# A hybrid trunk step: the copies of the first expert matrix in pieces of 1 MB that begin behind the memory's keys and values, and these keys and values in panels of 512 columns

## The chip, the cores and the metric

The kernel runs on one core of a Trainium2 chip. A core has five engines that run in parallel, each with its own order of instructions: TensorE (PE in the profile; its loads of the standing operand are PEld), VectorE (DVE), ScalarE (ACT), GpSimd (POOL) and SyncE (SP), and 16 DMA engines that they feed through queues. The metric is the device time of one execution in microseconds, less is better. Engines wait for each other by semaphores; a DMA that is issued from an engine's queue (SPq, ACTq, POOLq) stands in that engine's order like any other instruction, so what stands behind it waits as long as the issue does.

## The reference

One layer of a trunk, in float32, for a prompt of 256 tokens and 8 samples of 8 tokens (64 tokens), which share all weights. D is 2048.

```
mk, mv = mem_kv(mem_prompt, norm_mem_kv, w_mem_k, w_mem_v)    # 256 memory tokens: rmsnorm, then @ wk and @ wv
m = mixer(rmsnorm(x), ...)                                    # h = xn @ w_in; SSD scan, short convolution; @ w_out
x = x + m
x = x + mem_attend(rmsnorm(x), mem_k, mem_v, w_mem_q, w_mem_o)  # 4 heads of 512
x = x + peer(rmsnorm(x), w_peer_q, sub_keys, peer_u, peer_v)    # 8 heads, best 16 of 128 x 128 experts
```

The prompt attends to the keys and values that `mem_kv` has just made (they are outputs too); each sample attends to its own cached ones (`cache_mem_k`, `cache_mem_v`, 256 tokens each). In `peer` every token takes 128 of 16384 experts: `act = gelu(x . u[e])`, and the result is the sum of `g * act * v[e]`. `peer_u` and `peer_v` are 16384 x 2048 matrices, 134 MB each.

## The kernel before

**Arithmetic.** A matrix product in float32 is made of three matmuls of a rounded type (fp32r): each operand is split into a high part H and the rest L, and H*H, L*H and H*L are summed in PSUM. The split of a weight tile of 128x512 is one ScalarE instruction (`split`, L233: H is the rounded copy) and one VectorE subtraction (L234: L). So a unit of weights goes from DRAM into a room, through ScalarE, through VectorE, and then into 12 matmuls or so.

**The stages** follow each other along one stream: memory keys and values (two GEMMs of 256 tokens by 2048x2048), the input projection `w_in` with the SSD scan and the short convolution among it, the output projection `w_out`, the memory queries and attention over memory, `w_mem_o`, the queries of the experts (`w_peer_q`), the stage that multiplies all tokens with all of `peer_u`, and the stage that does the same with `peer_v`. TensorE, VectorE and ScalarE follow the order in which the program writes their instructions.

**The stream** (class `Stream`). A unit of work goes through four steps: its load is issued; three units later (WA) it is prepared, which is its split; it stands in a queue of up to six units (GD; four for units of attention, KVB - 1); and it is popped, which writes its matmuls. With every pop the stream also takes one step of a generator `steady` (L521), and a number of steps, by a rate, of each side job (norms, scans, softmax). So the units of the GEMMs set the place of all other work. There are four rooms of 512 KB for weight loads (WB; all weight loads are issued by SyncE) and seven buffers each for H and L (HLB).

**The keys and values** (L523 to L533). Each of the two matrices is done in 8 panels of 256 columns. A panel is 8 units; a unit takes two of the 16 row blocks k of the weight, and a load of 512 KB serves two units (rows of 1 KB, L293 to L300; the first two rooms are filled ahead, L402). The memory tokens are the standing operand here (`tok=True`): for each of 2 blocks of tokens and 2 blocks k there are three matmuls of 128x256 (L312 to L314). At the end of a panel two evictions by ScalarE (L530) scale the rows into a tile of 256 KB, and GpSimd issues the DMA that stores it (L532). During the first units a side job `mem_in` at rate 1.5 (L437) transposes and splits the memory tokens. In all there are 128 units.

**The copies.** `ordered_rows` (L509 to L519) copies `peer_u` into a DRAM buffer `u_d`, with its elements in another order: 512 copies of 256 KB each, DRAM to DRAM, issued from ScalarE's queue (L518), in pieces of 2 KB (512 columns). `u_d[i]` holds the 128 experts of row i, so that 32 partitions hold a quarter of the columns, and the stage that reads it can make its transpose by VectorE's 32x32 blocks. The copies begin after 48 pops, and then go at 0.92 of a copy for each pop. What is left at the end of attention is issued at once (`drain(strm.steady)`). The stage that reads them takes `u_d[i]` (1 MB, contiguous, 8 KB per partition) by one DMA of SyncE for each of 128 rows (L1760).

**Attention.** For each of 4 heads there are 8 key tiles of the samples and one of the prompt, and as many value tiles. A key tile comes by four DMAs of SyncE in pieces of 512 B (L1199), a value tile by one DMA of GpSimd (L1202), into four buffers (KVT); tiles are fetched three ahead. VectorE turns key tiles (L1223), ScalarE makes the high part (KH, L1232), VectorE or GpSimd the rest (KL, L1233). Units of `w_mem_q` and `w_mem_o` stand between the units of attention.

**Semaphores of the DMAs.** The DMAs that SyncE and ScalarE issue share eight semaphores (DMAHW0 to DMAHW7 in the orders below), taken in turn in the order in which the program writes the DMAs. A DMA that takes a semaphore again carries a wait for the landing of the one before it there, eight back, unless its engine has seen that landing already.

Of the kernel before, what the change touches and what calls it, by code (L numbers as in the profile page):

```python
# [11 lines left out]
F32 = mybir.dt.float32  # L12
# [3 lines left out]
AF = mybir.ActivationFunctionType  # L16
# [3 lines left out]
P = 128  # L20
D = 2048
KC = D // P
TP = 256
# [109 lines left out]
def wait(n):  # L133
    for _ in range(n):
        yield 1
# [11 lines left out]
def step(ctx, tc, ins, outs, dbg=None, stop=None):  # L147
# [23 lines left out]
    def ps(name="ps"):  # L171
        return psp.tile([P, 512], F32, tag="ps", name=name)
# [38 lines left out]
    def wfree(w):  # L211
        for r in rooms:
            if r[1] is w:
                r[1:] = None, next(turn)
# [16 lines left out]
    def split(h, l, src):  # L231

        S.activation(h, src, AF.Copy)  # L233
        V.tensor_tensor(l, src, h.bitcast(F32), ALU.subtract)  # L234
# [34 lines left out]
    def gain(j, k):  # L269
        return GAIN[:, 16 * j + k:16 * j + k + 1]  # L270

    def gemm(w2d, col0, ncol, ah, al, n, evac, ktot=KC, row0=0, tok=False, w0=None):


        nm = n // P if tok else (ncol + P - 1) // P
        pts = []
        box = {}

        def unit(kq):
            def load():  # L280
                if kq in (0, 2) and w0 is not None:
                    box["room", kq + 1] = w0[kq // 2]
                    box["w"] = w0[kq // 2].rearrange("p (k n) -> p k n", n=ncol)
                elif kq % 2 == 0:
                    w = box["room", kq + 1] = wtile(box["room", kq - 1] if kq % 4 else None)
                    wv = w[:, 0:4 * ncol].rearrange("p (k n) -> p k n", n=ncol)
                    r0 = row0 + kq * 2 * P
                    nc.sync.dma_start(wv, w2d[r0:r0 + 4 * P, col0:col0 + ncol].rearrange("(k p) n -> p k n", p=P))
                    box["w"] = wv
                box["w", kq] = box["w"]  # L290

            def prep():
                h, l = high(), low()  # L293
                hv = h[:, 0:2 * ncol].rearrange("p (k n) -> p k n", n=ncol)
                lv = l[:, 0:2 * ncol].rearrange("p (k n) -> p k n", n=ncol)
                q = kq % 2
                split(hv, lv, box.pop(("w", kq))[:, 2 * q:2 * q + 2])
                if q == 1:
                    wfree(box.pop(("room", kq)))
                box[kq] = (hv, lv)  # L300

            def comp():
                if kq == 0:
                    pts.extend(ps(f"pg{m}") for m in range(nm))
                hv, lv = box.pop(kq)
                for m in range(nm):
                    for j in range(2):
                        k = kq * 2 + j
                        st, sp = k == 0, k == ktot - 1
                        if tok:  # L310
                            out, a0, a1 = pts[m][:, 0:ncol], ah[:, k, m * P:(m + 1) * P], al[:, k, m * P:(m + 1) * P]
                            PE.matmul(out, a0, hv[:, j], start=st, stop=False)  # L312
                            PE.matmul(out, a0, lv[:, j], start=False, stop=False)
                            PE.matmul(out, a1, hv[:, j], start=False, stop=sp)  # L314
                        else:
                            c0, c1 = m * P, min(ncol, m * P + P)
                            out = pts[m][0:c1 - c0, 0:n]
                            PE.matmul(out, hv[:, j, c0:c1], ah[:, k, 0:n], start=st, stop=False)  # L318
                            PE.matmul(out, hv[:, j, c0:c1], al[:, k, 0:n], start=False, stop=False)  # L319
                            PE.matmul(out, lv[:, j, c0:c1], ah[:, k, 0:n], start=False, stop=sp)  # L320
# [77 lines left out]
    for i in range(2):  # L398
        for b in range(2):
            cols = slice(1024 * i, 1024 * i + 1024)  # L400
            nc.sync.dma_start(mem[b][:, cols], mem_prompt[0, b * P:(b + 1) * P, cols])
        nc.sync.dma_start(w0[i], w_mem_k[0, 512 * i:512 * i + 512, 0:256].rearrange("(k p) n -> p k n", p=P))  # L402
    squares = [pM.tile([P, 4], F32, name=f"sq{b}") for b in range(2)]

    def half_square(b, i):
# [28 lines left out]
        half_square(b, 0)  # L434
    next(mi)
    next(mi)
    strm.side(mi, 1.5)  # L437

    def x_norm():
        gb = gain_rows(norm_mix[0])  # L440
# [65 lines left out]
            yield 1  # L506
        S.activation(alog, alog, AF.Exp)

    def ordered_rows(first, last, share):  # L509

        n, done_ = 0, 0.0
        for i in range(first, last):
            for b in range(4):
                while done_ < 1:
                    done_ += share
                    yield 1
                done_ -= 1
                nc.scalar.dma_start(u_d[i, 32 * b:32 * b + 32].rearrange("p (a d) -> p a d", a=4),  # L518
                                    peer_u[0, i * P:(i + 1) * P, 512 * b:512 * b + 512].rearrange("(a p) d -> p a d", p=32))  # L519

    strm.steady = chain(wait(48), ordered_rows(0, P, 0.92))  # L521
    side = strm.side(chain(x_norm(), vectors(), histories()), 0.3)
    for w, dst in ((w_mem_k, p_mem_k), (w_mem_v, p_mem_v)):  # L523
        d2 = dst[0, 0].rearrange("m h d -> m (h d)")
        for c in range(8):
            def evac(m, pt, c=c, d2=d2, box={}):
                if m == 0:
                    box["o"] = pM.tile([P, 2, 256], F32, tag="kvo", bufs=2, name="kvo")
                o = box["o"]
                S.activation(o[:, m], pt[:, 0:256], AF.Copy, scale=mem_scale[m])  # L530
                if m == 1:
                    nc.gpsimd.dma_start(d2[:, c * 256:(c + 1) * 256].rearrange("(m p) n -> p m n", p=P), o)  # L532
            gemm(w[0], c * 256, 256, MH, ML, TP, evac, tok=True, w0=w0 if w is w_mem_k and c == 0 else None)  # L533
    strm.then(lambda: drain(side))
    strm.then(strm.sides.clear)
    strm.then(pMs.close)
# [1522 lines left out]
```

## Time and profile before

| | |
|---|---|
| median of 3 runs | 3337.76 us (3334.13 to 3353.14) |
| the profiled execution | 3339.66 us, its span 3338.0 us |
| mean granted TensorE clock | 0.982 |
| busy: TensorE, VectorE, ScalarE, GpSimd | 96%, 72%, 49%, 41% of the span |
| keys and values | some 11 to 242 us |
| input and output projection | some 242 to 1250 us |
| memory queries and attention | some 1250 to 1530 us |
| stage that reads `u_d` | some 1760 to 2608 us |
| copies into `u_d` | issued from 115.0 to 1243.4 us |

The profile's page gives the busy time of each engine, and then the span in 40 equal slices (83 us each) with a digit for the busy tenths of each. A row of windows gives the busy time of each engine in one stretch, the granted clock, the busy share of the 16 DMA engines, and GB/s. A row of the timeline is one instruction: its start, its duration, the engine, the line, what it writes and reads, and in brackets how long its engine was idle before and what ended that. A row of the waits sums, for two kinds of instructions, how long one waited for the other: total, times, longest. Matmuls are pipelined, so that the spacing of their starts and not their duration is what each costs.

### The profile page before, as it was taken

The numbers are of one execution on the slowest core, as the hardware profiler recorded it, in microseconds if no ns is written. First come the engines' busy times: TensorE is split into PE (matmuls) and PEld (weight loads), VectorE is DVE, ScalarE is ACT, GpSimd is POOL, SyncE is SP. The second block draws the span as 40 slices with busy tenths as digits, with TensorE's granted clock in tenths as the row PEclk, the third lists the DMA queues.
The fourth block names the chain that finished last, engine by engine and source line by source line (L and its number), as shares of the span: only waits on it lengthen the run. The fifth ranks groups of instructions, "written<-read, shape, count | busy, mean of one in ns | idle before, by whom it ended". The sixth has DMA issues, their size and how long they took to land. (4 is left out here: it accounts for less than half of the span.)

```text
span 3338.0 us, 59412 instructions
## 1 busy us (share of the span) xinstructions
PE 3196.1 (96%) x21357; PEld 3006.4 (90%) x21357; DVE 2387.4 (72%) x4558; ACT 1641.4 (49%) x3235; POOL 1363.9 (41%) x1431
## 2 busy tenths in 40 slices
PE   6998999999999999989999989899999999999998
PEld 6998899999999999878999989899999887878886
DVE  4535676665566447776687899988886688878886
ACT  4544453333355345555444444366665454545554
POOL 0001121111100001231127988888888555656652
PEclk8998999999999999989999999999999999999999
DMA  8897788988799889676686577787899899999996
GB/s 200 263 328 249 227 277 275 288 273 270 250 321 291 278 290 228 188 227 209 169 217 219 188 287 282 262 310 280 316 328 317 284 333 330 337 320 333 339 312 203
DMA packets 497652, 909.43 MB, mean 272 GB/s; under 512 B 46767, under 2 KB 325447, under 8 KB 471844
## 3 DMA queue, kind: packets, MB, share of 16 engines
q1 hardware_dynamic: 369068, 562.95, 51.2%
q0 software_dynamic: 54560, 208.44, 18.7%
q10 hardware_dynamic: 73728, 134.25, 13.2%
q8 instruction: 167, 2.74, 0.3%
q14 instruction: 129, 1.06, 0.1%
HBM read 849.40 MB, written 190.05 MB: 311 GB/s over the span
## 5 line engine op out<-in xcount | busy, mean ns | idle before, releaser
L234 DVE TENSOR_TENSOR L<-W,H 128x512 fp32r<-128x512 f32 x1320 | 909.9, 717 | 392.5 <-ACT H L233 376.8
L233 ACT ACTIVATE H<-W 128x512 fp32r<-128x512 f32 x1320 | 802.9, 625 | 756.0 <-PE acc L1962 264.7
L1790 POOL TENSOR_TENSOR L<-tt,H 128x512 fp32r<-128x512 f32 x490 | 630.3, 1315 | 94.2 <-ACT H L1787 83.8
L318 PE MATMUL pg<-AH,H 128*128 128x320 f32 (+1 forms) x1872 | 592.5, 316 | 19.7 <-ACT H L233 19.7
L1808 PE MATMUL pu<-XP,L 128*128 128x256 f32 x2048 | 586.7, 286 | 25.0 <-POOL L L1790 22.6
L1806 PE MATMUL pu<-XP,H 128*128 128x256 f32 x2048 | 588.8, 288 | 4.0 <-ACT H L1787 4.0
L320 PE MATMUL pg<-AH,L 128*128 128x320 f32 (+1 forms) x1872 | 584.0, 312 | 1.6 <-DVE L L234 1.5
L1807 PE MATMUL pu<-XP,H 128*128 128x256 f32 x2048 | 582.5, 284 | 0.0
L319 PE MATMUL pg<-AL,H 128*128 128x320 f32 (+1 forms) x1872 | 582.2, 311 | 0.0
L1808 PEld LDWEIGHTS pu<-XP,L 128*128 128x128 f32 x2048 | 395.5, 193 | 31.0 <-POOL L L1790 27.6
L1778 DVE STREAM_TRANSPOSE tt<-W 128x512 f32<-128x512 f32 x512 | 338.3, 691 | 105.2 <-POOL L L1790 99.6
L1787 ACT ACTIVATE H<-tt 128x512 fp32r<-128x512 f32 x512 | 309.9, 626 | 203.0 <-DVE tt L1778 186.5
L1961 PE MATMUL acc<-L,wt 128*128 128x512 f32 x1024 | 401.0, 392 | 6.9 <-DVE L L234 6.9
L1960 PE MATMUL acc<-H,wt 128*128 128x512 f32 x1024 | 400.4, 391 | 3.0 <-ACT H L233 3.0
L1806 PEld LDWEIGHTS pu<-XP,H 128*128 128x128 f32 x2048 | 396.4, 194 | 5.0 <-ACT H L1787 4.8
L1962 PE MATMUL acc<-H,wt 128*128 128x512 f32 x1024 | 400.3, 391 | 0.0
L1807 PEld LDWEIGHTS pu<-XP,H 128*128 128x128 f32 x2048 | 396.1, 193 | 0.0
L318 PEld LDWEIGHTS pg<-AH,H 128*128 128x128 f32 (+1 forms) x1872 | 354.3, 189 | 26.7 <-ACT H L233 22.3
L320 PEld LDWEIGHTS pg<-AH,L 128*128 128x128 f32 (+1 forms) x1872 | 353.6, 189 | 5.9 <-DVE L L234 5.1
L319 PEld LDWEIGHTS pg<-AL,H 128*128 128x128 f32 (+1 forms) x1872 | 354.4, 189 | 2.2
L1909 POOL TENSOR_TENSOR at<-at,G 128x108 f32<-128x108 f32 x192 | 173.2, 915 | 256.4 <-DMA at<-act_d 198.8
L1961 PEld LDWEIGHTS acc<-L,wt 128*128 128x128 f32 x1024 | 193.4, 189 | 49.8 <-DVE L L234 9.3
(487 smaller groups left out, 5706.2 us busy)
## 6 DMA issues: line engine op xcount, KB each, us to landing
u_d<-in_peer_u_dram ACTq DMA_DIRECT2D x512, 256.0 KB, 6.2
W<-u_d SPq DMA_DIRECT2D x128, 1024.0 KB, 5.3
W<-in_peer_v_dram SPq DMA_DIRECT2D x256, 512.0 KB, 7.1
W<-in_w_in_dram SPq DMA_DIRECT2D x176, 512.0 KB, 7.2
W<-in_w_out_dram SPq DMA_DIRECT2D x64, 512.0 KB, 7.1
W<-in_w_mem_k_dram SPq DMA_DIRECT2D x32, 512.0 KB, 5.0
W<-in_w_mem_v_dram SPq DMA_DIRECT2D x32, 512.0 KB, 8.4
W<-in_w_mem_q_dram SPq DMA_DIRECT2D x32, 512.0 KB, 7.0
```

The source lines that it names most:

```text
L233: S.activation(h, src, AF.Copy)
L234: V.tensor_tensor(l, src, h.bitcast(F32), ALU.subtract)
L318: PE.matmul(out, hv[:, j, c0:c1], ah[:, k, 0:n], start=st, stop=False)
L319: PE.matmul(out, hv[:, j, c0:c1], al[:, k, 0:n], start=False, stop=False)
L320: PE.matmul(out, lv[:, j, c0:c1], ah[:, k, 0:n], start=False, stop=sp)
L1790: G.tensor_tensor(l, src, h.bitcast(F32), ALU.subtract)
L1806: PE.matmul(pu[:, 0:TP], hv[:, j], PP["xp"][:, 0, k], start=k == 0, stop=False)
L1807: PE.matmul(pu[:, 0:TP], hv[:, j], PP["xp"][:, 1, k], start=False, stop=False)
L1808: PE.matmul(pu[:, 0:TP], lv[:, j], PP["xp"][:, 0, k], start=False, stop=k == KC - 1)
L1960: PE.matmul(out, th, h, start=i == 0, stop=False)
L1961: PE.matmul(out, th, l, start=False, stop=False)
L1962: PE.matmul(out, tl, h, start=False, stop=i == P - 1)
```

## The change

There are three edits. The keys and values are made in panels of 512 columns by a function of their own, `tokens_gemm`: 4 panels a matrix of 16 units, one k each, so again 128 units. A unit has 6 matmuls of 128x512, a load is two k of 512 columns (512 KB, rows of 2 KB), an eviction is 128x512, each with a store of 256 KB (16 in all, as before). The side job `mem_in` goes at half the rate. The copies are 128 of 1 MB (four rows of experts at once, 512 columns, pieces of 2 KB as before); they begin after 144 pops, 16 behind the last unit of the keys and values, and go at 0.19 of a copy for each pop. And `u_d` holds four rows of experts beside each other, so that the read of a row takes pieces of 8 KB that lie 32 KB apart. The loads, the evictions and matmuls of `gemm` for all other products stay as they were.

```diff
+    def tokens_gemm(w2d, c, ah, al, evac, w0=None):
+        pts, box = [], {}
+        def unit(k):
+            def load():
+                if k % 2 == 0:
...
+                        w = wtile()
+                        nc.sync.dma_start(w.rearrange("p (k n) -> p k n", n=512),
+                                          w2d[k * P:(k + 2) * P, 512 * c:512 * c + 512].rearrange("(k p) n -> p k n", p=P))
...
+            def comp():
...
+                for m in range(2):
+                    a0, a1 = ah[:, k, m * P:(m + 1) * P], al[:, k, m * P:(m + 1) * P]
+                    PE.matmul(pts[m], a0, h, start=k == 0, stop=False)
+                    PE.matmul(pts[m], a0, l, start=False, stop=False)
+                    PE.matmul(pts[m], a1, h, start=False, stop=k == KC - 1)
+                if k == KC - 1:
+                    for m in range(2):
+                        evac(m, pts[m])
...
-    u_d = drp.tile([P, P, D], F32, name="u_d")
+    u_d = drp.tile([P // 4, P, 4 * D], F32, name="u_d")
...
-    strm.side(mi, 1.5)
+    strm.side(mi, 0.75)
...
-    def ordered_rows(first, last, share):
+    def ordered_rows(share):
...
-        for i in range(first, last):
+        for i in range(P // 4):
             for b in range(4):
...
-                nc.scalar.dma_start(u_d[i, 32 * b:32 * b + 32].rearrange("p (a d) -> p a d", a=4),
-                                    peer_u[0, i * P:(i + 1) * P, 512 * b:512 * b + 512].rearrange("(a p) d -> p a d", p=32))
-    strm.steady = chain(wait(48), ordered_rows(0, P, 0.92))
+                nc.scalar.dma_start(u_d[i, 32 * b:32 * b + 32].rearrange("p (a d) -> p a d", d=512),
+                                    peer_u[0, 512 * i:512 * i + 512, 512 * b:512 * b + 512].rearrange("(a p) d -> p a d", p=32))
+    strm.steady = chain(wait(144), ordered_rows(0.19))
...
-        for c in range(8):
-            def evac(m, pt, c=c, d2=d2, box={}):
...
+        for c in range(4):
+            def evac(m, pt, c=c, d2=d2):
+                o = pM.tile([P, 512], F32, tag="kvo", bufs=2, name="kvo")
+                S.activation(o, pt, AF.Copy, scale=mem_scale[m])
+                nc.gpsimd.dma_start(d2[m * P:m * P + P, 512 * c:512 * c + 512], o)
+            tokens_gemm(w[0], c, MH, ML, evac, w0=w0 if w is w_mem_k and c == 0 else None)
...
-        nc.sync.dma_start(xt, u_d[i])
+        nc.sync.dma_start(xt, u_d[i // 4, :, D * (i % 4):D * (i % 4) + D])
```

TensorE, the first unit of the keys and values, before (pg are PSUM banks, one per block of 128 tokens; MH and ML are the two parts of the memory tokens):

```order
L312 MATMUL pg_190<-H,MH 128x256
L313 MATMUL pg_190<-L,MH 128x256
L314 MATMUL pg_190<-H,ML 128x256
L312 MATMUL pg_190<-H,MH 128x256
L313 MATMUL pg_190<-L,MH 128x256
L314 MATMUL pg_190<-H,ML 128x256
L312 MATMUL pg_191<-H,MH 128x256
L313 MATMUL pg_191<-L,MH 128x256
L314 MATMUL pg_191<-H,ML 128x256
```

and in the changed kernel, where L301 to L303 are the matmuls of `tokens_gemm`:

```order
L301 MATMUL pg_190<-H,MH 128x512
L302 MATMUL pg_190<-L,MH 128x512
L303 MATMUL pg_190<-H,ML 128x512
L301 MATMUL pg_191<-H,MH 128x512
L302 MATMUL pg_191<-L,MH 128x512
L303 MATMUL pg_191<-H,ML 128x512
```

A bank now takes three matmuls in a unit, of twice the columns, where it took six.

ScalarE, the end of the keys and values and the first units of the input projection, before (REP is a small table that is made between the two stages; an H is the high part of a weight tile; what an instruction waits for stands in brackets):

```order
L555 ACTIVATE REP<-ident 64x256 [waits Pool_49]
L518 DMA u_d<-in_peer_u_dram 128x1x512 [waits DMAHW2_49]
L233 ACTIVATE H<-W 128x64 [waits DVE_49]
L518 DMA u_d<-in_peer_u_dram 128x1x512 [waits DMAHW3_49]
L233 ACTIVATE H<-W 128x64 [waits DVE_49]
L518 DMA u_d<-in_peer_u_dram 128x1x512 [waits DMAHW5_49]
L233 ACTIVATE H<-W 128x64 [waits DVE_49,PE_49]
L518 DMA u_d<-in_peer_u_dram 128x1x512 [waits DMAHW6_49]
L233 ACTIVATE H<-W 128x512 [waits DVE_49,PE_49]
```

and in the changed kernel, in the same place:

```order
L584 ACTIVATE REP<-ident 64x256 [waits Pool_49]
L233 ACTIVATE H<-W 128x64 [waits DVE_49]
L233 ACTIVATE H<-W 128x64 [waits DMAHW0_49,DVE_49]
L233 ACTIVATE H<-W 128x64 [waits DVE_49,PE_49]
L233 ACTIVATE H<-W 128x512 [waits DMAHW1_49,DVE_49,PE_49]
L233 ACTIVATE H<-W 128x512 [waits DVE_49,PE_49]
L233 ACTIVATE H<-W 128x512 [waits DMAHW2_49,DVE_49,PE_49]
```

Before, a copy with a wait for a landing stands ahead of each split; now none stands there, and the splits wait for their own weights. Over the whole program 487 of the 512 copies of before carry such a wait, and 69 of the 128 new ones.

ScalarE, the keys of the last head in attention, before (tt is a turned key tile, kv a value tile; L1124 writes the queries of the samples):

```order
L1124 ACTIVATE qm<-qs 128x4x4x8
L1232 ACTIVATE KH<-tt 128x512 [waits DVE_49]
L1232 ACTIVATE KH<-tt 128x512 [waits DVE_49,PE_49] x2
L1232 ACTIVATE KH<-kv 128x512 [waits DMASW7_49,PE_49]
L1232 ACTIVATE KH<-tt 128x512 [waits DVE_49,PE_49,Pool_49]
L1232 ACTIVATE KH<-kv 128x512 [waits PE_49,Activation_49]
L1232 ACTIVATE KH<-tt 128x512 [waits DVE_49,PE_49,Activation_49]
```

and in the changed kernel (L1153 and L1261 are the same two lines):

```order
L1153 ACTIVATE qm<-qs 128x4x4x8
L550 DMA u_d<-in_peer_u_dram 512x1x512 [waits DMAHW6_49]
L1261 ACTIVATE KH<-tt 128x512 [waits DVE_49]
L1261 ACTIVATE KH<-tt 128x512 [waits DVE_49,PE_49] x2
L1261 ACTIVATE KH<-kv 128x512 [waits DMASW7_49,PE_49]
L1261 ACTIVATE KH<-tt 128x512 [waits DVE_49,PE_49,Pool_49]
L1261 ACTIVATE KH<-kv 128x512 [waits PE_49,Activation_49]
L550 DMA u_d<-in_peer_u_dram 512x1x512 [waits DMAHW3_49]
```

All 512 copies of before stand ahead of the first key tile of attention. Of the 128 new ones 91 do; the other 37 stand among the tiles of attention, each with a wait for a landing.

More of the change, by code (lines that the diff above doesn't have):

```diff
@@ L270, in gain, with prep, gemm @@
         return GAIN[:, 16 * j + k:16 * j + k + 1]
-    def gemm(w2d, col0, ncol, ah, al, n, evac, ktot=KC, row0=0, tok=False, w0=None):
-        nm = n // P if tok else (ncol + P - 1) // P
+    def tokens_gemm(w2d, c, ah, al, evac, w0=None):
[3 more added lines that the diff above has]
+                if k % 2 == 0:
+                    if w0 is not None and k < 4:
+                        w = w0[k // 2]
+                    else:
+                        w = wtile()
+                        nc.sync.dma_start(w.rearrange("p (k n) -> p k n", n=512),
+                                          w2d[k * P:(k + 2) * P, 512 * c:512 * c + 512].rearrange("(k p) n -> p k n", p=P))
+                    box["room", k + 1] = box["w"] = w
+                box["w", k] = box["w"][:, 512 * (k % 2):512 * (k % 2) + 512]
+            def prep():
+                h, l = high(), low()
+                split(h, l, box.pop(("w", k)))
+                if k % 2:
+                    wfree(box.pop(("room", k)))
+                box[k] = h, l
+            def comp():
+                if k == 0:
+                    pts.extend(ps(f"pg{m}") for m in range(2))
+                h, l = box.pop(k)
+                for m in range(2):
[6 more added lines that the diff above has]
+                        evac(m, pts[m])
+            strm.add(load, None, prep, comp)
+        for k in range(KC):
+            unit(k)
+    def gemm(w2d, col0, ncol, ah, al, n, evac, ktot=KC, row0=0):
+        nm = (ncol + P - 1) // P
         pts = []
@@ L280, in load @@
             def load():
[L281 to L284, printed above, removed]
+                if kq % 2 == 0:
                     w = box["room", kq + 1] = wtile(box["room", kq - 1] if kq % 4 else None)
@@ L309, in comp @@
                         st, sp = k == 0, k == ktot - 1
[L310 to L320, printed above, removed]
+                        c0, c1 = m * P, min(ncol, m * P + P)
+                        out = pts[m][0:c1 - c0, 0:n]
+                        PE.matmul(out, hv[:, j, c0:c1], ah[:, k, 0:n], start=st, stop=False)
+                        PE.matmul(out, hv[:, j, c0:c1], al[:, k, 0:n], start=False, stop=False)
+                        PE.matmul(out, lv[:, j, c0:c1], ah[:, k, 0:n], start=False, stop=sp)
                 if kq == ktot // 2 - 1:
@@ L401, in step @@
             nc.sync.dma_start(mem[b][:, cols], mem_prompt[0, b * P:(b + 1) * P, cols])
-        nc.sync.dma_start(w0[i], w_mem_k[0, 512 * i:512 * i + 512, 0:256].rearrange("(k p) n -> p k n", p=P))
+        nc.sync.dma_start(w0[i], w_mem_k[0, 256 * i:256 * i + 256, 0:512].rearrange("(k p) n -> p k n", p=P))
     squares = [pM.tile([P, 4], F32, name=f"sq{b}") for b in range(2)]
@@ L507, in histories @@
         S.activation(alog, alog, AF.Exp)
-    def ordered_rows(first, last, share):
-        n, done_ = 0, 0.0
-        for i in range(first, last):
+    def ordered_rows(share):
+        done_ = 0.0
+        for i in range(P // 4):
             for b in range(4):
@@ L524, in step @@
         d2 = dst[0, 0].rearrange("m h d -> m (h d)")
-        for c in range(8):
-            def evac(m, pt, c=c, d2=d2, box={}):
[L527 to L533, printed above, removed]
+        for c in range(4):
[4 more added lines that the diff above has]
+            tokens_gemm(w[0], c, MH, ML, evac, w0=w0 if w is w_mem_k and c == 0 else None)
     strm.then(lambda: drain(side))
```

## The prediction

> **What bounds the kernel now.** I read the page first (span, slices, queues, DMA issues), then a table of windows by stage, then the timeline of TensorE for the spacing of its matmuls, then the waits inside the stages that the change touches.
>
> ```profile
> span 3338.0 us, 59412 instructions
> ...
> PE   6998999999999999989999989899999999999998
> ...
> DMA  8897788988799889676686577787899899999996
> ...
> q10 hardware_dynamic: 73728, 134.25, 13.2%
> ...
> u_d<-in_peer_u_dram ACTq DMA_DIRECT2D x512, 256.0 KB, 6.2
> W<-u_d SPq DMA_DIRECT2D x128, 1024.0 KB, 5.3
> ```
>
> TensorE is busy in nearly every slice, so a stage gets shorter only where its matmuls take fewer slots or where a wait of TensorE ends earlier. The DMA row is the other thing to see: slices 2 to 14 (83 us each) carry the copies into u_d, slices 15 to 19 carry none. q10 is ScalarE's queue, the copies alone: 13.2% of 3338 us on all 16 DMA engines is 440 us for 512 copies, 0.86 us for 256 KB and 3.44 us for 1 MB.
>
> The windows, one per stage (busy us and instructions of each engine, granted clock, DMA share, GB/s): memory keys and values, the change to the input projection, its first part, the rest up to the end of the output projection, attention before and after its value tiles begin, and the stage that reads u_d.
>
> ```profile
> 40.00:242.00 202.00, 197.46 (x1626) 193.84 (x1626) 102.89 (x185) 103.79 (x201) 10.68 (x15) 0.99 0.87 280
> 242.00:262.00 20.00, 16.11 (x89) 13.85 (x88) 7.03 (x13) 6.84 (x15) 3.04 (x9) 0.84 1.02 348
> ...
> 300.00:460.00 160.00, 146.61 (x972) 141.33 (x971) 102.89 (x202) 79.32 (x164) 25.63 (x80) 0.97 0.76 245
> 460.00:1250.00 790.00, 785.32 (x5437) 769.83 (x5436) 466.58 (x949) 337.39 (x616) 82.38 (x177) 1.00 0.89 282
> 1265.00:1350.00 85.00, 80.11 (x542) 77.94 (x541) 60.27 (x117) 46.10 (x95) 9.76 (x8) 0.96 0.85 204
> 1350.00:1520.00 170.00, 149.86 (x902) 130.45 (x901) 135.01 (x218) 98.26 (x202) 57.06 (x59) 0.93 0.76 217
> ...
> 1760.00:2600.00 840.00, 809.63 (x6656) 802.30 (x6656) 712.04 (x1502) 449.98 (x981) 719.81 (x568) 0.99 0.78 278
> ```
>
> From 40 us on the keys and values are bound by TensorE alone. From 300 to 460 us it has holes. From 1350 to 1520 us, in attention, it is busy for only 150 of 170 us, VectorE for 135, and the DMA engines already work 76% of the time with no copy among their work.
>
> **The change part by part: the panels.** The keys and values go from 1536 matmuls of 256 columns to 768 of 512. The spacing of each is in the timeline: 18 matmuls of the old kind in a row, and 28 of 512 columns from the last stage, which also loads a new 128x128 operand for each.
>
> ```profile
> 99.78 0.28 PE L312 MATMUL pg<-H,MH 128*128 128x256 f32 x1
> ...
> 101.82 0.28 PE L314 MATMUL pg<-H,ML 128*128 128x256 f32 x1
> ```
>
> ```profile
> 3049.73 0.39 PE L1961 MATMUL acc<-L,wt 128*128 128x512 f32 x1
> ...
> 3055.85 0.39 PE L1961 MATMUL acc<-L,wt 128*128 128x512 f32 x1
> ```
>
> 17 steps in 2.04 us are 0.120 us each; 27 steps in 6.12 us are 0.2267 us. Two old ones against one new one: 0.240 - 0.2267 = 0.0133 us, times 768 = 10.2 us, nearly all of it after 40 us, where 1626 matmuls by 0.12 us fill 195 of 202 us. **Term 1: -10.2 us.**
>
> The Trainium skill (TensorE: Matmul & The Clock Gate, section on the back-to-back issue gap) gives a warm gap of N/2.4 + 2.5 ns, that is 109.2 ns for 256 columns and 215.8 ns for 512. By that the panels would save 768 x 2.5 ns = 1.9 us, and the sum below would be 8.3 us higher, about 3336 us. The trace does not agree: both spacings lie 11 ns above the page's, so the fixed part is 13.3 ns per matmul, and I go by the rows.
>
> Edits of this part at nothing: the loads keep 512 KB, and 2 KB rows replace 1 KB ones; the splits keep their count and shape; 32 evictions become 16 wider ones on ScalarE, busy for 104 of 202 us; the transposes of the memory run at half the rate per unit, and a unit now needs one k instead of two. If ScalarE's slack were gone, an eviction would cost some tenths of a us, 16 times.
>
> **The copies leave the keys and values.** ScalarE waited there for late weights, and TensorE did not notice, since six units lie ready ahead of it:
>
> ```profile
> ACT H L233 <- DMA W<-in_w_mem_v_dram: 28.0, 14, 3.7
> ```
>
> The 197 busy of 202 us leave 5 us, of which a share comes back. **Term 2: -2 us (0 to -4).** At the change to the input projection the cover fails, since the units of its first panel are short:
>
> ```profile
> 253.40 0.31 PE L320 MATMUL pg<-AH,L 128*128 128x320 f32 x1
> 257.32 0.63 PE L318 MATMUL pg<-AH,H 128*128 128x320 f32 x1 [3.62 <-ACT H L233]
> ```
>
> ```profile
> 255.99 0.55 ACTq L518 DMA_DIRECT2D u_d<-in_peer_u_dram  x1
> 256.64 0.63 ACT L233 ACTIVATE H<-W 128x512 fp32r<-128x512 f32 x1 [5.53 <-DMA W<-in_w_in_dram]
> ```
>
> The split that TensorE waits for starts 0.65 us after a copy was issued: the copy stands ahead of it in ScalarE's queue and itself waits for a landing. The DMA share there is 1.02. With no copy before pop 149 both go: 3.6 us, and 1 to 2 us at the lower clock (0.84) behind the gap. **Term 3: -5 us (-2 to -7).**
>
> **The copies in the projections.** Their rate falls from 0.92 x 256 KB to 0.19 x 1 MB for each unit, by 17%, and the issues from 512 to 128. In the order of ScalarE 487 of the old copies carry a wait for a landing; of the new ones 69 do, 37 of those in attention. Between 240 and 460 us TensorE waits for splits that stand behind copies or late weights:
>
> ```profile
> ACT H L233 <- DMA W<-in_w_in_dram: 22.9, 7, 5.5
> ...
> PE pg L318 <- ACT H L233: 14.8, 7, 5.6
> ```
>
> 14.8 us less the 3.6 of term 3 leave 11.2. What is late next is the chain of the convolution on VectorE, which feeds the same ScalarE, so I take 8 us and 1 for the clock. **Term 4: -9 us (0 to -13).** From 460 to 1250 us TensorE is busy for 785 of 790 us; nothing is taken there. 384 issues fewer by 0.55 us leave ScalarE 211 us, which it did not lack (337 busy of 790).
>
> **The copies in attention.** This is what the change adds. 37 copies of 1 MB now fall behind the first key tile, between some 1280 and 1520 us, where there were none. They meet loads that arrive just in time:
>
> ```profile
> L1199 SPq DMA_DIRECT2D kv<-in_cache_mem_k_dram x128: 311/448/1307, 1266.2 to 1479.7; - x128
> ...
> DMA to landing us min/median/max: 2.8/4.3/6.6
> ```
>
> ```profile
> ACT KH L1232 <- DMA kv<-in_cache_mem_v_dram: 2.5, 2, 2.2
> ```
>
> Upper bound: 37 x 3.44 = 127 us of DMA work on top of 0.85 x 85 + 0.76 x 170 = 201 us, 328 us in a stretch of 255 us, +73 us if DMA bound it fully. Lower bound 0: the copies fill the 54 idle us, the busy share falls under a mixed load, and the tiles' four buffers take up the rest. Below 0 nothing: no wait of this stage goes. The nearest row is the 28.0 us that ScalarE waited for weights in the keys and values, at a DMA share near 1, while these copies passed:
>
> ```profile
> L518 ACTq DMA_DIRECT2D u_d<-in_peer_u_dram x73: 548/550/1602, 115.0 to 241.5; - x73
> ```
>
> That is 0.4 us a copy. 37 x 0.4 = 15, and here nothing lies ready to cover it. In ScalarE's order each of the 37 waits for a landing and has a split of a tile behind it, for which TensorE, and VectorE's subtraction, wait. **Term 5: +16 us (0 to +73).**
>
> **At nothing in the stage that reads u_d:** the reads become 8 KB pieces 32 KB apart. A load lands in 5.3 us, one is wanted every 840/128 = 6.6 us, and three double rooms take them ahead. If it took twice as long the cover would be thin, and each further us would cost up to 128 us.
>
> **The sum.** The profiled execution took 3339.66 us: its span of 3338.0 and 1.7 around it; the median of the runs is 3337.76, 1.9 less. 3339.7 - 10.2 - 2 - 5 - 9 + 16 = 3329.5; against the median 3327.6, so 3328 us. About 0.5%, 16.7 us, is what a measurement of this kernel can tell from no change.
>
> **The rivals.** First, the copies vanish in the gaps of attention. For it: 0.76 of the DMA time is an average with some windows lower, and tiles are fetched three ahead. Against it: the value tiles' waits above show no reserve. Then terms 1 to 4 stand alone: 3337.8 - 26.2 = 3312 us, faster.
>
> Second, attention becomes bound by DMA. The key tiles come as pieces of 512 B on SP's queue and the copies as pieces of 2 KB on ScalarE's; each tile is behind a copy, SP's next load waits for the copy's landing, and the tiles' buffers come free later. For it: 201 + 127 us of work in 255 us. Against it: the shares are measured under load, and the engines moved 348 GB/s in one window and 217 here. At 60% of the upper bound the loss is 45 us: 3337.8 - 26.2 + 45 = 3357 us, slower. It decides from a loss of 43 us on (26.2 + 16.7). The Trainium skill (DMA: Bandwidth & Descriptors, section on queues, rings and completion order) says that a DMA engine takes turns between the queues it has work for, a packet at a time. By that a tile of small pieces loses most to a queue of larger ones, which is this rival; no row of before shows the two together.
>
> Third, the stage that reads u_d slows by its 32 KB rows; 1 us a load beyond the reserve would be 3440 us. Nothing in the rows points to it: 1 in 50, within slower. That the copies do not move is excluded by the order.
>
> **How the numbers follow.** The forecast, a partial loss in attention, 0.39; no loss, 0.36; DMA-bound or slow reads, 0.25. The forecast is within 0.5%, the first rival faster, the others slower: 0.36, 0.39, 0.25. Low end: terms 1 to 4 at their best, 34 us, and no loss: 3303 us. High end: gains of 20 us and a loss of 50: 3368 us.
>
> **What would show it.** Right: spacing 0.227 us in the keys and values, which end 15 us earlier or more; no gap of TensorE at the first panel of the projection; half the waits for splits from there to the first 60 units; from 1280 to 1520 us a longer stretch, with waits of KH for kv tiles or of ScalarE ahead of KH. Wrong: the stretch of attention unchanged, or longer than all that was won; or loads of u_d landing later than 6.6 us.

## The result and the profile after

The changed kernel takes 3358.07 us (median of 5 runs, 3353.86 to 3365.99), before 3339.71 us (5 runs): the ratio is 1.0051, with a 95% interval of 1.0027 to 1.0076. That is half a per cent slower, where 3328 us and no change beyond the noise was forecast. The profiled execution took 3354.43 us, its span is 3352.7 us. The page of the changed kernel, in the rows that answer to those of before:

```profile
span 3352.7 us, 57522 instructions
...
PE   6999999999999998779999998899999999999998
...
DMA  8666788787888889997586577787899899999996
...
q10 hardware_dynamic: 67584, 134.23, 12.1%
...
u_d<-in_peer_u_dram ACTq DMA_DIRECT2D x128, 1024.0 KB, 7.4
W<-u_d SPq DMA_DIRECT2D x128, 1024.0 KB, 6.2
```

TensorE's row now has two sevens in slices 16 and 17 (counted from 0), in attention, where the DMA row has nines. The DMA row fell to sixes in slices 1 to 3, the keys and values. The windows, the same stages as before (busy us and instructions of TensorE, its weight loads, VectorE, ScalarE and GpSimd, granted clock, DMA share, GB/s):

```profile
40.00:242.00 202.00, 197.14 (x950) 161.84 (x949) 111.61 (x201) 108.03 (x198) 11.07 (x24) 0.99 0.67 209
242.00:262.00 20.00, 19.04 (x134) 18.55 (x132) 17.04 (x34) 9.52 (x24) 2.96 (x9) 1.00 0.46 133
...
300.00:460.00 160.00, 157.49 (x1082) 153.61 (x1081) 114.36 (x233) 82.87 (x177) 27.61 (x90) 0.98 0.75 244
460.00:1250.00 790.00, 785.49 (x5437) 772.11 (x5436) 465.92 (x947) 336.38 (x614) 78.98 (x161) 1.00 0.83 264
1265.00:1350.00 85.00, 73.43 (x486) 69.65 (x484) 52.17 (x87) 36.21 (x73) 12.64 (x12) 0.92 1.02 306
1350.00:1520.00 170.00, 133.44 (x713) 111.87 (x712) 112.84 (x184) 82.35 (x171) 46.41 (x48) 0.82 1.01 314
...
1760.00:2600.00 840.00, 811.71 (x6642) 803.60 (x6641) 719.40 (x1554) 449.63 (x980) 707.93 (x559) 0.99 0.78 278
```

In attention the DMA share went from 0.85 and 0.76 to 1.02 and 1.01, and TensorE's part of its time fell. For the length of each stage I use landmarks: the small table REP that ScalarE makes at the end of the keys and values, the high parts KH of the first and the last tile of attention, and the first read of the copies. Each row has the first and the last start of its kind. Before:

```profile
L555 ACT ACTIVATE REP<-ident x1: 409/409/409, 241.6 to 241.6; 64x256 f32<-64x256 f32 x1
```

```profile
L1232 ACT ACTIVATE KH<-tt x72: 614/632/699, 1281.5 to 1495.3; 128x512 fp32r<-128x512 f32 x72
L1232 ACT ACTIVATE KH<-kv x72: 614/620/644, 1353.9 to 1529.8; 128x512 fp32r<-128x512 f32 x72
```

```profile
L1760 SPq DMA_DIRECT2D W<-u_d x128: 319/320/573, 1744.8 to 2579.2; - x128
```

After:

```profile
L584 ACT ACTIVATE REP<-ident x1: 402/402/402, 228.2 to 228.2; 64x256 f32<-64x256 f32 x1
```

```profile
L1261 ACT ACTIVATE KH<-tt x72: 613/632/682, 1248.2 to 1506.5; 128x512 fp32r<-128x512 f32 x72
L1261 ACT ACTIVATE KH<-kv x72: 613/624/656, 1333.0 to 1547.8; 128x512 fp32r<-128x512 f32 x72
```

```profile
L1789 SPq DMA_DIRECT2D W<-u_d x128: 319/320/1514, 1763.3 to 2598.1; - x128
```

The same landmarks for every run, from its own profiled execution (us, from unrounded times, so the last digit can differ by 0.1 from the rows above; the median and the ratio are those of the timed runs against before in the same session):

| run | keys and values end | projections (to the first KH) | attention (first to last KH) | to the first read | median | ratio, 95% interval |
|---|---|---|---|---|---|---|
| before | 241.6 | 1039.9 | 248.3 | 215.0 | 3339.71 | |
| changed | 228.2 | 1020.0 | 299.6 | 215.5 | 3358.07 | 1.0027 to 1.0076 |
| panels alone | 236.1 | 1039.1 | 249.2 | 215.7 | 3331.25 | 0.9965 to 0.9993 |
| copies at 0.28 | 229.9 | 1028.5 | 250.8 | 215.5 | 3316.23 | 0.9926 to 0.9952 |
| copies at 0.23 | 229.0 | 1025.4 | 279.6 | 213.7 | 3338.84 | 0.9990 to 1.0020 |
| small copies | 229.2 | 1024.6 | 322.7 | 214.6 | 3381.03 | 1.0117 to 1.0150 |
| tiny in attention | 229.4 | 1020.7 | 251.6 | 216.4 | 3307.26 | 0.9874 to 0.9945 |
| small, tiny in attention | 229.2 | 1025.7 | 274.6 | 213.8 | 3333.92 | 0.9978 to 1.0013 |
| early, 1 MB | 234.6 | 1033.5 | 247.8 | 214.1 | 3329.59 | 0.9970 to 1.0001 |
| held in attention | 228.3 | 1023.8 | 252.1 | 229.4 | 3321.98 | 0.9943 to 0.9976 |
| old panels, at 0.28 | 237.3 | 1026.2 | 250.8 | 213.3 | 3321.79 | 0.9936 to 0.9965 |
| two rates | 229.3 | 1011.9 | 251.3 | 216.3 | 3303.45 | 0.9872 to 0.9911 |
| two rates, held | 229.1 | 1025.3 | 249.9 | 216.3 | 3310.22 | 0.9897 to 0.9926 |
| no copies | 229.5 | 1006.9 | 248.6 | 214.6 | 3294.6 | 0.9839 to 0.9877 |

How far do such lengths repeat? The changed kernel and the run with tiny copies have the same program up to attention, and so do the two runs with small copies: their projections agree within 1.1 us (1020.0 and 1020.7, 1024.6 and 1025.7). Attention without copies lies between 247.8 and 252.1 us in nine runs. The totals vary more: the timed runs of one kernel spread by 5 to 23 us, and a profiled execution lay up to 10 us from its median.

The second row accounts for the change: 13.4 us won in the keys and values, 19.9 in the projections, 51.3 lost in attention, 0.5 behind it. The sum is +18.5 us at the first read of the copies; at the end of the span it is +14.7. The 4 us between the two lie in stages that the change does not touch, within the spread of the totals.

### The profile page after: what moved, and what is told of

It is laid out like the page before. It is cut to its first block, busy times and chain, and to the rows that moved or that the text cites. A ratio compares the mean times of both kernels' runs of the same rounds, so it can differ in the third digit from the quotient of the medians.

```text
span 3352.7 us, 57522 instructions
## 1 busy us (share of the span) xinstructions
PE 3194.9 (95%) x20589; PEld 2971.7 (89%) x20589; DVE 2391.4 (71%) x4558; ACT 1634.0 (49%) x3219; POOL 1364.5 (41%) x1431
## 3 DMA queue, kind: packets, MB, share of 16 engines
q10 hardware_dynamic: 67584, 134.23, 12.1%
q14 instruction: 125, 1.02, 0.1%
## 5 line engine op out<-in xcount | busy, mean ns | idle before, releaser
L350 PEld LDWEIGHTS pg<-AH,H 128*128 128x128 f32 (+1 forms) x1872 | 353.1, 189 | 16.5 <-ACT H L233 12.2
L1990 PEld LDWEIGHTS acc<-L,wt 128*128 128x128 f32 x1024 | 193.2, 189 | 46.5 <-DVE L L234 6.8
```

The source lines that it names most:

```text
L1990: PE.matmul(out, th, l, start=False, stop=False)
```

## The experiments

Theory A: the copies put more work on the DMA engines in attention than these have time for, so the bytes decide. Theory B: a copy in ScalarE's order waits for a landing and holds the splits of tiles behind it, so the number of copies decides. Theory C: the loss comes from the panels, or from what they shift.

**Panels alone** (the changed kernel with the old `ordered_rows`, start, rate and layout).

```diff
...
-    strm.steady = chain(wait(144), ordered_rows(0.19))
+    strm.steady = chain(wait(48), ordered_rows(0, P, 0.92))
...
```

> The panels of 512 columns alone, with the 512 old copies of 256 KB from pop 48 at 0.92 and the old layout of the buffer. In the changed kernel the keys and values ended 13.4 us earlier (241.6 to 228.2 us), and the stretch from the first to the last high part of a key or value tile in attention went from 248.3 to 299.6 us. Theory A (the copies' DMA work in attention is the whole loss): here that stretch is as before, 248 us within 4; the keys and values end 10 to 13 us earlier; the total is 10 to 13 us under before. Theory C (the loss comes from the panels or from what they shift, not from copies in attention): the stretch grows by 20 us or more and the total is over before.

Attention is as before (249.2), the projections too (1039.1). C falls. The keys and values gain 5.5 us, half of what was expected, and the total 7 us (0.9979 of before).

**All copies ahead of attention.**

```diff
-    strm.steady = chain(wait(144), ordered_rows(0.19))
+    strm.steady = chain(wait(144), ordered_rows(0.28))
```

> The changed kernel with the copies at 0.28 for each pop in place of 0.19: all 128 stand ahead of the first key tile, none in attention. Theory A: the stretch of attention falls back to 248 us within 5; the projections get up to 15 us longer by half as many copies again; the total is 36 to 51 us under the changed kernel, some 3307 to 3322 us. Theory C: the stretch stays at 290 us or more.

Attention is back at 250.8 us and the total 42 us under the changed kernel's: one number of the change made it a loss. The projections pay 8.5 us for the higher rate.

**Half of them in attention.**

```diff
-    strm.steady = chain(wait(144), ordered_rows(0.19))
+    strm.steady = chain(wait(144), ordered_rows(0.23))
```

> The changed kernel with the copies at 0.23 for each pop: 18 copies of 1 MB stand in attention in place of 37, at its beginning. Theory A: a loss in proportion, 18/37 of 51 us, so a stretch of about 248 + 25 = 273 us, within 8, and a total 18 to 28 us under the changed kernel. If only the full DMA engines of the whole stretch cost and a part of it has room, the stretch is under 262 us.

18 copies cost 31 us (279.6 against 248.3), a little over their share. The windows of this run split attention where the copies end, at 1380 us:

```profile
1254.40:1380.00 125.60, 96.21 (x592) 89.82 (x590) 72.35 (x120) 50.29 (x104) 18.52 (x17) 0.86 0.98 310
1380.00:1534.00 154.00, 134.20 (x783) 114.70 (x784) 120.56 (x197) 91.50 (x190) 51.94 (x54) 0.92 0.77 219
```

The share is 0.98 while copies run and 0.77 behind them. The loss lies where the copies are. The engines' idle time behind 1380 us was of no use to them: at 2.6 to 2.9 us a copy (worked out below) 18 copies are 47 to 52 us of work, less than the 54 us that the whole stage had idle before.

**Small copies** (256 KB at 0.76 from pop 144, old layout): the same bytes, four times the number.

```diff
...
-    strm.steady = chain(wait(144), ordered_rows(0.19))
+    strm.steady = chain(wait(144), ordered_rows(0, P, 0.76))
...
```

> The changed kernel with copies of 256 KB at 0.76 from pop 144 and the old layout of the buffer: the same bytes at the same places, but four times as many copies in ScalarE's order; 147 copies in attention, each with a wait for a landing. Theory A (bytes decide): the stretch of attention is within 10 us of the changed kernel's 299.6. Theory B (each copy holds ScalarE up until a landing, and the tiles' splits behind it): four times as many waits, so the stretch gets longer by 30 us or more. In the projections, by both, four times the issues cost some us there, as in before: total 0 to 12 us over the changed kernel by A, 30 or more by B.

322.7 us lies between the two: 23 us more than with 37 large copies, where A asked for under 10 and B for 30 or more. So the next two runs take the bytes away and leave the order.

**Tiny copies in attention, in the changed kernel.**

```diff
-                nc.scalar.dma_start(u_d[i, 32 * b:32 * b + 32].rearrange("p (a d) -> p a d", d=512),
...
+                n = 32 if 4 * i + b < 91 else 1
+                nc.scalar.dma_start(u_d[i, 32 * b:32 * b + n].rearrange("p (a d) -> p a d", d=512),
...
```

> The changed kernel, where each of the 37 copies that stand in attention moves 32 KB in place of 1 MB; the other rows are read from the matrix itself, in its own order, so the last experts get wrong elements and the same work. The order of ScalarE and all its waits for landings stay. Theory A (the copies' DMA work): the stretch of attention falls from 299.6 to 250 us, within 5, and the total to 50 us under the changed kernel, within 8. Theory B (a copy holds ScalarE and the splits behind it): the stretch stays over 285 us.

The stretch is 251.6 us, among the runs without any copy in attention (247.8 to 252.1). So the 37 issues without their bytes cost some 3 us of the 51, no more than such runs differ by, and the bytes 48. The waits of this run in attention, and then those of the changed kernel (who waited for whom, us in total, times, longest):

```profile
ACT KH L1262 <- DVE tt L1253: 53.5, 47, 2.6
...
DVE KL L1263 <- ACT KH L1262: 16.2, 42, 2.3
```

```profile
ACT KH L1261 <- DVE tt L1252: 82.0, 50, 7.6
...
DVE KL L1262 <- ACT KH L1261: 30.9, 46, 5.3
...
DVE tt L1252 <- DMA kv<-in_cache_mem_k_dram: 21.1, 8, 5.2
...
ACT KH L1261 <- DMA kv<-in_cache_mem_v_dram: 18.7, 10, 6.4
...
DVE tt L1252 <- DMA kv<-out_dram: 10.7, 3, 7.1
```

With the bytes there, the turned tiles (tt) come late because their tiles (kv) land late, and the rest of the chain waits behind them. Tiny copies also land sooner, so this run takes away, with the bytes, the waits for landings that the bytes make long. The largest of these are not ScalarE's, whose splits of tiles waited 2.8 us for a copy, but those of SyncE, where a load of a key tile waits for a copy that has the same semaphore: in attention of the changed kernel, then with tiny copies:

```profile
SPq L1228 <- DMA u_d<-in_peer_u_dram: 33.2, 17, 7.1
```

```profile
SPq L1229 <- DMA u_d<-in_peer_u_dram: 11.3, 4, 7.3
```

How much of the 48 us passes through these waits is not separated. As the DMA engines were busy for the whole stretch (a share of 1.00, below), their work is the bound that the rows show, and not the later issue of a load.

**Tiny copies in attention, in the kernel with small copies** (the same edit, for its copies behind the first 365).

```diff
...
+                n = 32 if 4 * i + b < 365 else 1
+                nc.scalar.dma_start(u_d[i, 32 * b:32 * b + n].rearrange("p (a d) -> p a d", a=4),
...
```

> The kernel with small copies (256 KB at 0.76 from pop 144), where each of the 147 copies in attention moves 8 KB in place of 256 KB, and the other rows are read from the matrix itself, as in the run above. With all bytes the stretch of attention took 322.7 us, 23 us more than with a quarter as many copies of four times the size. If these 23 us are what 110 more issues and waits cost in ScalarE's order, the stretch is 249 + 20 to 35 = 270 to 285 us here; if they come from the DMA engines (more and shorter transfers in flight beside the tiles), it is 250 to 258 us.

274.6 us. With the runs above this makes a square: 37 copies 251.6 us without and 299.6 with their bytes, 147 copies 274.6 and 322.7. The bytes cost 48 us in both rows, and 110 more copies cost 23 in both columns, 0.2 us each. So A holds for the change: its 37 copies cost little beyond their bytes. The number of copies is a second, smaller price, which B in its own form (30 us or more) overstated. Whether those 0.2 us lie in ScalarE's waits, in its issues (0.55 us each) or in the semaphores that its copies share with SyncE's loads these runs don't separate. With 147 copies the DMA share over the stretch is 0.72 without the bytes and 0.95 with them, so there the engines are not quite full, and the bytes cost more than the work that exceeds the idle time (109 us added, 77 idle: 32, and 48 measured).

**Copies of 1 MB from pop 48.**

```diff
-    strm.steady = chain(wait(144), ordered_rows(0.19))
+    strm.steady = chain(wait(48), ordered_rows(0.23))
```

> The changed kernel with the copies of 1 MB from pop 48 at 0.23 for each pop, the old schedule in bytes; none stands in attention. The panels with the old copies gave: keys and values to 236.1 us, from there to the first key tile 1039.1 us, total 3331; 0.23 from pop 144 gave 229.0 and 1025.4 us. If it is the size of the pieces (fewer issues and waits in ScalarE's order) that frees the projections: 1025 to 1030 us, total 3318 to 3324. If it is the start (no copy at the change to the projection and in its first units): 1035 to 1040 us, total 3328 to 3334. In both cases the stretch of attention is 250 us, within 4.

The projections take 1033.5 us, between both. Beside the panels alone (1039.1) the larger pieces are worth 5.6 us; the later start at the same rate (1025.4) 8.1 more; the lower rate of the change (1020.0) another 5.4. So both causes that were offered have a part.

**Old panels, copies at 0.28** (the kernel before, with the copies and the layout of the changed kernel).

```diff
...
-    strm.steady = chain(wait(48), ordered_rows(0, P, 0.92))
+    strm.steady = chain(wait(144), ordered_rows(0.28))
...
```

> The old panels of 256 columns, with the copies of 1 MB from pop 144 at 0.28 (none in the keys and values, none in attention). So far the keys and values ended at 241.6 us in before, at 236.1 with the panels alone, and at 228 to 230 in six runs with both the panels and no copy beside them. If the panels are worth 10.2 us by the spacing of their matmuls and the copies beside them 2, they end at 239 to 240 us here; if the copies beside them cost what the difference of those runs says (6 to 8 us), at 234 to 236. The rest as in the run at 0.28: total 3316 and the 4 to 10 us that the panels save, 3320 to 3326.

The keys and values end at 237.3 us, between the two. So the panels are worth 7.4 us without copies beside them (to 229.9) and 5.5 with (241.6 to 236.1), and the copies' leaving 4.3 with the old panels and 6.2 with the new.

**Held in attention, the rest behind it** (the generator adds nothing to its count while attention runs, and what is left is issued ahead of the stage that reads the copies).

```diff
-                    done_ += share
+                    done_ += 0 if hold else share
...
-    strm.steady = chain(wait(144), ordered_rows(0.19))
+    hold = []
+    strm.steady = chain(wait(144), ordered_rows(0.225))
...
+    strm.then(lambda: hold.append(1))
     for _ in range(3):
         strm.then(next_load)
...
     strm.then(residual_in)
+    strm.then(hold.clear)
...
-    strm.then(lambda: drain(strm.steady))
...
+    strm.then(lambda: drain(strm.steady))
     for i in range(P):
```

> The changed kernel with the copies at 0.225 from pop 144, held while attention runs (from its first queries to the last value tile) and resumed in the output product and the queries of the experts, the rest issued before the stage that reads them: 105 copies ahead of attention, none in it, 23 behind. Theory A: projections as with 0.23 (1025 us), attention 250 us, the stretch from the last tile to the first read of the copies 215 us plus 0 to 10; total 40 to 52 us under the changed kernel, 3306 to 3318. If the later stages have no room for them, that stretch grows by 20 us or more (23 copies by 0.9 us or more).

Attention is 252.1 us, but 23 copies behind it cost 14 us (229.4 against 215.5), and the total of 3321.98 us lies over what was expected. The two windows of this run are the output product and the queries of the experts:

```profile
1504.00:1610.00 106.00, 104.59 (x707) 103.84 (x706) 62.96 (x112) 51.05 (x98) 3.06 (x5) 0.98 0.85 285
1610.00:1734.00 124.00, 112.02 (x776) 108.56 (x775) 85.43 (x297) 46.46 (x93) 31.29 (x66) 0.96 1.05 291
```

The loss is in the second, at a share of 1.05; the first has room.

**Two rates.**

```diff
...
-                    done_ += share
+                    done_ += 0 if hold else 0.12 if n < 106 else 0.33
+                    n += 1
...
```

> The changed kernel with the copies at 0.12 in the first 106 pops of the projection (up to some 430 us) and 0.33 behind them; none in attention. TensorE's spacing between 300 and 460 us exceeded the one of back-to-back matmuls by 21 us at 0.19 and by 29 at 0.28, and behind 460 us not even 0.28 cost anything. If only the convolution's stretch is sensitive: projections 1016 to 1021 us, attention 250, total 3304 to 3312. If 0.33 fills the DMA engines (their share was 0.92 at 0.28), the projections get longer than 1029 us.

Nothing is held here (`hold` stays empty). This beats both kernels: 3303.45 us, 0.9891 of before; the projections, 1011.9 us, are shorter than expected. Its windows are the convolution's stretch, the rest of the projections, and attention:

```profile
300.00:460.00 160.00, 160.00 (x1117) 156.43 (x1116) 116.18 (x237) 85.47 (x184) 29.32 (x93) 1.00 0.69 222
460.00:1204.00 744.00, 739.48 (x5117) 726.11 (x5116) 440.60 (x891) 311.64 (x572) 76.05 (x157) 1.00 0.95 328
1241.20:1492.50 251.30, 222.49 (x1390) 199.26 (x1389) 194.46 (x316) 141.24 (x292) 70.48 (x71) 0.95 0.75 211
```

From 460 us on the DMA engines work 95% of the time, and TensorE is busy for all but 4.5 of 744 us. In the run without copies (last of all) it is busy for all but 4.5 of 739 us there (460 to 1199 us), at a share of 0.54.

**Two rates, held in attention** (the holding as above).

```diff
...
-                    done_ += share
+                    done_ += 0 if hold else 0.1 if n < 106 else 0.3
+                    n += 1
...
```

> As the run with two rates, with 0.10 and then 0.30, held in attention, and 8 copies left for the output product behind it, where the DMA share was 0.53. Projections 1015 to 1021 us, attention 250, from the last tile to the stage that reads the copies 215 to 219 us, total 3304 to 3312. In the run with 23 copies behind attention that last stretch took 229 us, when copies met the loads of the keys of the experts; if 8 already cost over 5 us there, the room behind attention is no room.

The stretch behind attention is as with two rates (216.3), so 8 copies fit there. But the projections take 13 us more, which was not expected. The loss lies at the change to the memory queries: up to 1200 us TensorE does as much in both runs, and from 1204 to 1255 us it is busy for 46.5 of 51 us with 293 matmuls here, and for 49.5 with 340 with two rates. Here copies still stand in that place, as the copies between 1170 and 1260 us show, first of this run and then with two rates:

```profile
L551 ACTq DMA_DIRECT2D u_d<-in_peer_u_dram x10: 549/549/606, 1170.2 to 1232.8; - x10
```

```profile
L551 ACTq DMA_DIRECT2D u_d<-in_peer_u_dram x5: 549/549/550, 1170.0 to 1199.0; - x5
```

That these copies are the cause is not shown: the changed kernel has nine between 1173.0 and 1256.0 us, and TensorE is busy for 50.8 of 51 us there. The total is 7 us behind two rates.

**No copies.**

```diff
-    strm.steady = chain(wait(144), ordered_rows(0.19))
+    strm.steady = wait(1)
...
-        nc.sync.dma_start(xt, u_d[i // 4, :, D * (i % 4):D * (i % 4) + D])
+        nc.sync.dma_start(xt, peer_u[0, P * i:P * i + P])
```

> The changed kernel without any copy; the stage that reads them takes the rows from the matrix itself, in its own order, so the experts get wrong elements and the same work. What is left is the floor of what placing the copies can bring: keys and values to 228 us, projections 1012 to 1018, attention 248, total 3295 to 3305.

3294.6 us, with projections of 1006.9 us, shorter than expected. Two rates are within 9 us of this floor, the changed kernel 63 over it.

## Why the prediction was wrong

**Terms 1 and 2, the keys and values:** -12.2 forecast, -13.4 measured, but shared otherwise. The panels are worth 5.5 to 7.4 us and not 10.2, the copies' leaving 4.3 to 6.2 and not 2. The spacing came as forecast, in the timeline of the changed kernel:

```profile
101.64 0.39 PE L302 MATMUL pg<-L,MH 128*128 128x512 f32 x1
...
105.29 0.39 PE L303 MATMUL pg<-H,ML 128*128 128x512 f32 x1
```

16 steps in 3.65 us are 0.228 us each. So the price of a matmul was right, and the runs without copies beside the panels show what took the rest. From 40 us to the end of the keys and values TensorE is busy for 193.82 of 197.3 us with the old panels and for 183.36 of 189.9 with the new ones (both at 0.28): 10.5 us less busy, and 3.1 more idle. The idle time of the new ones is its wait for VectorE's normalized prompt (6.5 us in 2 waits, where the old panels have 1.8 in one), which a side job turns on TensorE among the units of the keys and values. The prediction has no term for it; why these waits grew no run shows. Term 2 was held to at most 4 us because TensorE was busy for 197 of 202 us; with the copies gone and the old panels kept, its busy time itself fell, from 197.1 to 193.8. An estimate by the fixed 2.5 ns that the Trainium skill gives for a single matmul (TensorE: Matmul & The Clock Gate, section on the back-to-back issue gap) would have made the panels worth 1.9 us; the measured 7.4 and 10.5 do not agree with it.

**Terms 3 and 4, the change to the projection and its first units:** -14 forecast, -19.9 measured for the whole projections. The window from 242 to 262 us is full now (19.0 busy of 20, clock 1.00), and the waits of TensorE for splits between 240 and 480 us fell from 14.8 to

```profile
PE pg L350 <- ACT H L233: 6.9, 2, 4.6
```

which is about the half that the prediction named as a sign. Its sum had taken more from these waits, 11.6 us, and they gave 7.9. The gain was larger because other things gave too: TensorE's idle time over the projections fell by 14.2 us in all (26.8 to 12.5), 3.3 of them in a wait for the scan's table DTT on VectorE (4.2 to 0.9), and its busy time for about the same records fell by 5.7 (1013.1 to 1007.5), while the granted clock between 228 and 460 us went from 0.95 to 0.98. So the place and the main cause were right, and the sizes were not. In the runs the changes of start, pieces and rate are worth 8.1, 5.6 and 5.4 us.

**The stage that reads the copies:** at nothing, and so it is. From its first read to the last it takes 834.4 us before (1744.8 to 2579.2) and 834.8 after (1763.3 to 2598.1), though a read now lands in 6.2 us and not 5.3.

**Term 5 is the step that failed:** +16 us (0 to +73), measured +51.3. The prediction took its value from "the 28.0 us that ScalarE waited for weights in the keys and values", 0.4 us a copy, and argued that each copy holds a split of a tile in ScalarE's order. That row is not the nearest. It comes from a stage with six units ready ahead, which TensorE bounds, and a wait on ScalarE there says little on a stage that the DMA engines bound. The run with tiny copies showed that the 37 issues in the order are worth some 3 us. The prediction's own upper bound was the right model: work against time. The windows from the first to the last KH, before and after:

```profile
1281.50:1529.80 248.30, 223.27 (x1383) 200.83 (x1382) 193.14 (x316) 141.35 (x292) 70.70 (x71) 0.94 0.78 213
```

```profile
1248.20:1547.80 299.60, 241.39 (x1381) 211.52 (x1380) 194.57 (x316) 141.40 (x292) 71.15 (x71) 0.85 1.00 310
```

Before, 0.78 x 248.3 = 194 us of DMA work left 54 us idle. After, all 299.6 us are work, 106 more, or 2.9 us for each of the 37 copies. That 106 less 54 makes the loss is no test yet, since both come from the same two windows. A price from another stage makes it one: the projections of two rates, with all 128 copies, and without copies:

```profile
229.30:1241.20 1011.90, 1002.84 (x6929) 982.46 (x6928) 623.85 (x1265) 452.05 (x871) 118.89 (x290) 0.99 0.88 298
```

```profile
229.50:1236.40 1006.90, 1000.96 (x6929) 980.77 (x6928) 626.13 (x1265) 453.18 (x872) 117.80 (x290) 1.00 0.55 167
```

0.88 x 1011.9 less 0.55 x 1006.9 are 337 us, 2.6 us a copy; the same sum for the changed kernel's 91 copies there (0.80 of 1020.0 us) gives 2.9. So 37 copies are 97 to 107 us of work, and less the 54 idle us they cost 43 to 53; 51.3 were measured. The prediction's 3.44 us a copy gave 73. The gaps were indeed filled, as the first rival had it, and they were filled to the last; the rest could only lengthen the stage.

**The rivals.** The second rival, attention bound by DMA, said 3357 us at 0.25, and the result is 3358. That it came so near is in part luck: its loss of 45 (60% of the upper bound, a share without a row) was 6 under the one measured, and the gains of 26.2 were 7 under the 33.3 measured, so that two errors cancel. Its mechanism shows in SyncE's waits for copies above, and in the landing of key tiles, which was 4.3 us in the median before:

```profile
DMA to landing us min/median/max: 3.8/7.5/11.2
```

The Trainium skill (DMA: Bandwidth & Descriptors, section on queues, rings and completion order) has a DMA engine take turns between its queues by packets. The longer landings agree with that, but full engines alone would lengthen them too, and no run here tells the two apart. The first rival, no loss, falls with the chance of 0.36 that it was given. The third, slow reads, falls too. The forecast of "the same" rested on term 5 alone: with 52 in place of 16 the sum of the prediction comes to 3328 + 36 = 3364 us, slower, and the larger gains bring it to the result.

## What to carry to other kernels

When work for a shared resource is moved into a stage, count that stage's idle time of the resource and the work that is added, and take what is left over as the first estimate: here 43 to 53 us by a price from another stage, against 51.3 measured. Count only the idle time in which that work can run (18 copies at the start of the stage lost 31 us with idle time behind them), and take the estimate as a lower one where the work comes in many small pieces (the bytes of 147 copies: 109 us into 77 idle cost 48 and not 32). A wait in another stage is no price for it, unless that stage has the same bound and the same cover. Background copies belong where TensorE is the bound and its operands lie ready (a DMA share of 0.95 cost nothing there), and their rate should follow the stages: one rate that ends too late lost 18 us, and two rates won 36.

## What the runs showed of the hardware

By the shares of the windows a copy of 1 MB, DRAM to DRAM, took 2.6 to 2.9 us of all 16 DMA engines. By its packets' time on the page of the changed kernel (12.1% of 3352.7 us for 128 copies) it took 3.2, so such a price belongs to one way of measuring. Beyond its bytes each further copy cost some 0.2 us, at 147 copies in 275 us. A DMA share of 0.95 cost a stage nothing in which TensorE was busy for 739.5 of 744 us. When attention became DMA-bound, the granted clock in it fell from 0.94 to 0.85, and TensorE's busy time for about the same records rose from 223 to 241 us; as it waited for tiles in any case, nothing shows that this cost time of its own.
